# Where the split weights begin in their buffers, in the feed forwards of a two-layer decoder trunk

## The chip, the core and the metric

The kernel runs on one core of a Trainium2 chip. The metric is the device time of one execution in microseconds; the figure for the kernel before is the median of three runs. In the text TensorE (PE in the profile) multiplies matrices, and loading its weights is shown apart (PEld); VectorE is DVE, ScalarE is ACT, GpSimd is POOL, SyncE is SP.

## The reference

One sequence of 512 tokens, width 1024, goes through two layers. The first mixes with a gated DeltaNet, the second with sliding-window attention; both also attend to 256 memory tokens. After the mixing, each layer has a gated feed forward of width 2816. All in float32.

```python
def swiglu(h, w_gate_up, w_down):
    gu = h @ w_gate_up
    return (jax.nn.silu(gu[..., :D_FF]) * gu[..., D_FF:]) @ w_down

def reference(x, mem, ...):
    mem_n = rms_norm(mem, ln_mem)
    for layer in range(DEPTH):
        h = rms_norm(x, ln_mix[layer])
        mkv = mem_n @ w_mem_kv[layer]
        ...
        x = x + jnp.concatenate([mix_out.astype(x.dtype), mem_o.astype(x.dtype)], axis=-1) @ w_out[layer]
        x = x + swiglu(rms_norm(x, ln_ffn[layer]), w_gate_up[layer], w_down[layer])
        ...
    return rms_norm(x, ln_final)
```

## The kernel before, in words

**A product in three matmuls.** Every float32 operand of a large product is split into a high part and the rest (`split`, L168: ScalarE copies the high part into a float32r tile, L140, and VectorE subtracts it, L153). `mm3` (L198) then issues three matmuls for a tile of 128 by 128 weights: high weights by high inputs, high weights by the inputs' rest, the weights' rest by high inputs. In the profile they read `g<-h,whi`, `g<-l,whi`, `g<-h,wlo`: the moving operand first (the inputs, `h` and `l`, or `T`), then the weights. Each matmul loads its own weights (LDWEIGHTS in PEld).

**Where weights lie.** `weight` (L182) takes a block of weights that SP's queue has loaded into `wraw`, and splits it into a `whi` and a `wlo` tile of the pool `w`. `part` (L195) allots these with 1024 + 128 elements each, 128 more than a block fills. A block of eight tiles begins at the tile's first byte.

**The feed forward.** `ffn` (L1099) goes over the 22 pairs of gate and up columns in two halves of 11, and after each half multiplies the 11 results by the down weights. The first column of a half is done plainly with 512-wide matmuls (`projected`, `gate`). The others are done two at a time by `quarters` (L1275): one step of a fast method (Strassen-Winograd) over two blocks of columns, two halves of the input width and two halves of the tokens, seven products in place of eight. Each product is four tiles of weights times 256 tokens, so 4 × 3 = 12 matmuls that are 256 wide; their inputs are the normalised activations (`h`, `l`) or sums of them that were prepared at the start (`T`). VectorE forms the sums of weights and combines the results; GpSimd's queue adds weights to each other by accumulating DMAs. There are 19 calls of `quarters` in each feed forward, 1596 matmuls.

Their split weights come from `ring` (L1130): six places, each half of a `whi` and of a `wlo` tile, taken in turn. A place is 512 + 128 elements long, of which a product uses 512, beginning at element `shift[0]`. `begin` (L1139), which starts each call of `quarters`, sets `shift[0]` to `P - 8`, 120 elements or 480 bytes.

**The last rows.** In the second layer's last half the last two of eight blocks of rows are held back (`tail`), and done for 256 tokens at a time, so that normalising and storing the first half of the tokens runs beside the second half's products: 2 blocks × 2 halves × 11 tiles × 3 = 132 matmuls, 256 wide. Their weights are split to the beginning of `whi` and `wlo` tiles for the one block, of `T` tiles for the other.

**Positions.** In the built program each partition's `h`, `l` and `T` operands begin at 320 bytes beyond a multiple of 512, and so do `whi` and `wlo`; a further tile of weights is 512 bytes further on. The distance from the beginning of the weights to the beginning of the inputs, modulo 512, is therefore the same for all matmuls of a kind:

| matmuls | width | inputs beyond weights, bytes modulo 512 |
|---|---|---|
| quarter products, both feed forwards (3192) | 256 | 32 |
| last rows (132) | 256 | 0 |
| plain projections, all layers | 512 | 0 |
| memory keys, at the start (`mh`, `ml` as inputs, `whi` as weights) | 256 | 384 |
| memory values, at the start, with the roles exchanged (`whi` moving, `mh` as weights) | 256 | 128 or 416 |

The order of the work is that of the code; TensorE's instructions are issued in this order, and a place in the ring is written again when the matmuls that read it are done.

Of the kernel before, what the change touches and what calls it, by code (L numbers as in the profile page):

```python
# [18 lines left out]
P = 128  # L19
T = 512  # L20
D = 1024
KD = D // P
# [64 lines left out]
class Builder:  # L87
# [91 lines left out]
        self.loaded = self.nc.sync.dma_start(raw, src).ins  # L179
        return raw  # L180

    def weight(self, src, eng=None, raw=None, parts=1, pool=None, tags=("whi", "wlo"), bufs=3, after=None):  # L182

        raw = self.load(src) if raw is None else raw
        n = raw.shape[1]
        hi, lo = (self.part(tag, bufs, pool)[:, :n] for tag in tags)
        for i in range(parts):
            s = slice(i * n // parts, (i + 1) * n // parts)
            self.split(raw[:, s], hi[:, s], lo[:, s], eng or self.weng)
            if after is not None:  # L190
                for ins, other in zip((self.copied, self.low), after):
                    self.nosync(ins, other)
        return hi, lo
# [905 lines left out]
    def ffn(self, fp, xp, layer, h, apool, rope=False):  # L1099
# [4 lines left out]
        acts, sums, open_pairs, places, waiting, shift, sized = [], [], [], [], [], [0], []  # L1104
# [34 lines left out]
        def begin(f, up, by, tag, bufs, then):  # L1139

            o = [self.t(fp, [P, T], F32, tag, bufs) for _ in range(2)]
            steps = self.quarters(fp, [col(f + i, up) for i in range(2)], sums, by, o, ring)
            shift[0] = P - 8
            next(steps)
            while waiting:
                x = waiting.pop()
                self.nosync(self.fn(x, x, AF.Silu), self.held)
            end()
            next(steps)
            open_pairs.append((steps, then, o))  # L1150
            return o

        def end():
            if open_pairs:
                steps, then, o = open_pairs.pop()
                next(steps, None)
                for x in o:
                    then(x)

        def add(x, ps):  # L1160
            d = ps
            if not layer:
                d = self.t(fp, [P, T], F32, "fu", 3)
                self.tt(nc.vector, d, ps, self.rstd, ALU.mult)
            self.tt(nc.vector, x, d, x, ALU.add)

        for f0 in (0, half):
# [7 lines left out]
            for f in range(f0 + 1, f0 + half, 2):  # L1175
                if f == 1:
                    g = []
                    for i in range(2):
                        for _ in range(2 - i):
                            sums.append(self.token_sums(fp, layer, len(sums), h))  # L1180
                        g.append(gate(f + i))
                    sums.append(self.token_sums(fp, layer, len(sums), h))
                else:
                    g = begin(f, 0, (self.rstd, self.rstd), "fg", 4, lambda x: self.fn(x, x, AF.Silu))
                begin(f, 1, g, "fu", 3, put)
            end()
            self.acc = self.floor if layer else None
            tail = KD - 2 if f0 and layer else KD
            down = lambda m, j, n, **kw: self.weight(a["wdn"][layer, m][:, (f0 + j) * P:(f0 + j + n) * P], **kw)
            for m in range(tail):  # L1190
# [3 lines left out]
                for j, n in ((0, 6), (6, 5)):  # L1194
                    w = down(m, j, n)
# [7 lines left out]
        if tail < KD:  # L1203

            parts = (slice(0, T // 2), slice(T // 2, T))
            own = dict(pool=fp, tags=("T", "T"), bufs=8)
            w = {m: [down(m, j, n, **(own if m == KD - 1 else {})) for j, n in ((0, 6), (6, 5))] for m in range(tail, KD)}
            outs = [[self.t(fp, [P, D], F32, "T", 8) for _ in range(2)] for t in parts]
            for o, t in zip(outs, parts):
                for k in range(tail):  # L1210
                    self.put_row(o, k, self.x[k][:, t])
            ends = []
            for t in parts:
                acc = self.acc[:, t]
                for m in range(tail, KD):
                    ps, x = self.bank("pj")[:, :T // 2], self.x[m][:, t]
                    seeded = t.start > 0 and m == KD - 1
                    if seeded:
                        self.copy(ps, x)
                    for k in range(half):  # L1220
                        act = [part[:, t] for part in acts[k]]
                        self.mm3(ps, w[m][k // 6], k % 6, act, k == 0 and not seeded, k == half - 1, seeded)
                    if seeded:
                        x = ps
                    else:
                        add(x, ps)
                    if m < KD - 1:
                        sq = self.t(fp, [P, T], F32, "fg", 4)[:, t]
                        self.square(sq, x)
                        self.put_row(outs[len(ends)], m, x)  # L1230
                        nxt = self.t(xp, [P, T], F32, "sqa", 2)[:, t]
                        self.tt(nc.vector, nxt, acc, sq, ALU.add)
                        acc = nxt
                ends.append(self.final(fp, acc, x, outs[len(ends)], t, P if seeded else t.stop))
            for n, (end, o) in enumerate(zip(ends, outs)):
                self.store(*end, o, n)
# [381 lines left out]
```

## Time and profile before

| | |
|---|---|
| median of 3 runs | 1131.22 us (1130.96 to 1131.48) |
| the profiled execution | 1131.15 us, span 1129.4 us |
| TensorE, busy | 1119.9 us (99%) |
| weight loads, busy | 986.1 us (87%) |
| VectorE, busy | 827.6 us (73%) |
| ScalarE, busy | 634.4 us (56%) |
| granted TensorE clock | 0.998 |

The span runs from the first instruction to the last. A busy share is that of the whole span; matmuls are pipelined, so that one begins while the one before is still under way, and the length that a row gives for one matmul (some 280 ns for 256 columns) is longer than the distance from its beginning to the next one's beginning. What a matmul costs is this distance, called its spacing or step below; it is read from the length of a row in the chain of waits divided by its count, or from beginnings in the timeline.

### The profile page before, as it was taken

What the parts mean: (1) busy time and instruction counts of PE and PEld (TensorE: products, weight loads), DVE (VectorE), ACT (ScalarE), POOL (GpSimd) and SP (SyncE); (2) the same over time, 40 slices, a digit from 0 to 9 for tenths busy, and PEclk for the clock granted to TensorE, in tenths of its full rate; (3) what the DMA queues carried; (4) which work ended last, traced back from release to release, by engine and by line L of the source; (5) the groups of instructions that cost most, each with busy time, mean ns of one, the idle gap of its engine ahead of it and who ended that gap; (6) DMA issues with size and microseconds to landing.
All of it is one profiled execution on the core that took longest, in us unless ns stands there. A gap on an engine that the chain in (4) does not pass through costs nothing.

```text
span 1129.4 us, 19330 instructions
## 1 busy us (share of the span) xinstructions
PE 1119.9 (99%) x7339; PEld 986.1 (87%) x7339; DVE 827.6 (73%) x1553; ACT 634.4 (56%) x1285; POOL 73.2 (6%) x91
## 2 busy tenths in 40 slices
PE   9999999999999999999999999999999999999997
PEld 8888778887899988899988887788999988999986
DVE  7676976577888975588955877839999634889643
ACT  8588664456566632366643555856666422666434
POOL 0000000000021001011000000000111000111001
PEclk9999999999999999999999999999999999999999
DMA  8344252234567536377533321116687533776232
GB/s 314 109 153 149 95 131 86 85 113 145 174 167 195 143 111 169 102 191 195 134 89 102 132 75 38 53 43 180 158 201 185 144 103 105 173 190 156 77 103 87
DMA packets 72401, 151.15 MB, mean 134 GB/s; under 512 B 16956, under 2 KB 18516, under 8 KB 72308
## 3 DMA queue, kind: packets, MB, share of 16 engines
q1 hardware_dynamic: 60884, 129.21, 36.3%
q0 software_dynamic: 11136, 20.45, 11.2%
q8 instruction: 57, 0.93, 0.3%
q14 instruction: 36, 0.29, 0.1%
q10 hardware_dynamic: 288, 0.26, 0.1%
HBM read 142.94 MB, written 6.96 MB: 133 GB/s over the span
## 4 chain that ended last, share of the span: by engine, by line
PE 96%; DVE 2%; ACT 1%; DMA 0%; issue 0%; DVEq 0%; SPq 0%; ACTq 0%
PE pj L146 46%; PE g L146 38%; PE sc L146 6%; PE qk L146 3%; PE pt L146 2%; PE pt L150 1%; PE g L150 1%; DVE big L153 1%; DVE qv L156 0%; DVE btmp L153 0%; DMA early<-in_early 0%; DVE wlo L153 0%; ACT sm L134 0%; DVE T L153 0%; DVE gcr L153 0%
## 5 line engine op out<-in xcount | busy, mean ns | idle before, releaser
L140 ACT ACTIVATE whi<-wraw 128x512 fp32r<-128x512 f32 (+3 forms) x318 | 235.3, 748 | 240.6 <-PE pj L146 164.0
L153 DVE TENSOR_TENSOR wlo<-wraw,whi 128x512 fp32r<-128x512 f32 (+3 forms) x318 | 262.8, 837 | 92.7 <-ACT whi L140 85.2
L146 PE MATMUL pj<-h,whi 128*128 128x512 f32 (+1 forms) x652 | 256.4, 395 | 0.0
L146 PE MATMUL pj<-l,whi 128*128 128x512 f32 (+1 forms) x652 | 254.4, 390 | 0.0
L146 PE MATMUL pj<-h,wlo 128*128 128x512 f32 (+1 forms) x652 | 254.0, 390 | 0.0
L146 PE MATMUL g<-T,whi 128*128 128x256 f32 x1216 | 216.8, 279 | 0.0
L146 PEld LDWEIGHTS g<-T,whi 128*128 128x128 f32 x1216 | 185.1, 188 | 1.3 <-DVE fu L156 1.3
L146 PE MATMUL g<-T,wlo 128*128 128x256 f32 x608 | 169.7, 279 | 0.0
L146 PEld LDWEIGHTS pj<-h,whi 128*128 128x128 f32 x652 | 122.4, 188 | 28.0 <-issue 4.1
L146 PEld LDWEIGHTS pj<-h,wlo 128*128 128x128 f32 x652 | 122.5, 188 | 25.4 <-issue 0.9
L146 PE MATMUL g<-l,whi 128*128 128x256 f32 (+1 forms) x500 | 144.5, 289 | 0.0
L146 PE MATMUL g<-h,whi 128*128 128x256 f32 (+1 forms) x500 | 144.4, 289 | 0.0
L146 PE MATMUL g<-h,wlo 128*128 128x256 f32 (+1 forms) x500 | 144.4, 289 | 0.0
L146 PEld LDWEIGHTS pj<-l,whi 128*128 128x128 f32 x652 | 122.6, 188 | 23.6 <-DVE l L1468 0.3
L146 PEld LDWEIGHTS g<-T,wlo 128*128 128x128 f32 x608 | 114.3, 188 | 0.0
L146 PEld LDWEIGHTS g<-h,whi 128*128 128x128 f32 x500 | 94.0, 188 | 1.9
L146 PEld LDWEIGHTS g<-l,whi 128*128 128x128 f32 x500 | 93.9, 188 | 1.9
L146 PEld LDWEIGHTS g<-h,wlo 128*128 128x128 f32 x500 | 93.9, 188 | 1.8
L1286 POOL DMA_DIRECT2D ws<-in_wgu x38 | 33.5, 881 | 733.0 <-DMA ws<-in_wgu 399.1
L140 ACT ACTIVATE whi<-ws 128x512 fp32r<-128x512 f32 x76 | 48.0, 631 | 42.0 <-PE g L146 35.6
L153 DVE TENSOR_TENSOR wlo<-ws,whi 128x512 fp32r<-128x512 f32 x76 | 52.0, 684 | 5.9 <-ACT whi L140 5.9
L1287 POOL DMA_DIRECT2D ws<-in_wgu x38 | 34.2, 900 | 196.4 <-DVE wlo L153 71.4
(421 smaller groups left out, 1683.2 us busy)
## 6 DMA issues: line engine op xcount, KB each, us to landing
wraw<-in_wgu SPq DMA_DIRECT2D x50, 512.0 KB, 4.4
ws<-in_wgu SPq DMA_DIRECT2D x76, 256.0 KB, 3.4
ws<-in_wgu POOLq DMA_DIRECT2D x76, 256.0 KB, 4.5
wraw<-in_win SPq DMA_DIRECT2D x26, 512.0 KB, 3.6
wraw<-in_wdn SPq DMA_DIRECT2D x32, 384.0 KB, 3.1
wraw<-in_wdn SPq DMA_DIRECT2D x32, 320.0 KB, 2.9
wraw<-in_wgu SPq DMA_DIRECT2D x38, 256.0 KB, 4.0
wraw<-in_wout SPq DMA_DIRECT2D x16, 512.0 KB, 3.6
```

Source lines behind the costliest of these rows:

```text
L140: self.copied = self.nc.scalar.activation(out, in_, AF.Copy, **kw).ins
L146: return self.nc.tensor.matmul(out, lhsT, rhs, start=start, stop=stop, skip_group_check=more).ins
L150: return self.nc.tensor.transpose(out, in_, self.ident[:k, :k]).ins
L153: return eng.tensor_tensor(out=out, in0=a, in1=b, op=op).ins
L1286: nc.gpsimd.dma_start(s1, a22, accum_op=ALU.add)
L1287: nc.gpsimd.dma_start(s3, a21, accum_op=ALU.add)
```

## The change

The quarter products' weights begin elsewhere in their place of the ring: at element 80 (byte 320) in the first layer's feed forward and at element 16 (byte 64) in the second's, in both cases in place of element 120 (byte 480). `weight` gets an argument `at`, the element of the tile at which the split weights begin; the last rows' weights begin at element 80 in place of 0. So the inputs lie 192 bytes beyond the weights in the first feed forward (32 before), 448 in the second (32 before), and 192 in the last rows (0 before), modulo 512. The order of all engines' instructions and of the DMAs, their number and sizes, and the places of all other operands are the same as before.

```diff
-    def weight(self, src, eng=None, raw=None, parts=1, pool=None, tags=("whi", "wlo"), bufs=3, after=None):
+    def weight(self, src, eng=None, raw=None, parts=1, pool=None, tags=("whi", "wlo"), bufs=3, after=None, at=0):
 
         raw = self.load(src) if raw is None else raw
         n = raw.shape[1]
-        hi, lo = (self.part(tag, bufs, pool)[:, :n] for tag in tags)
+        hi, lo = (self.part(tag, bufs, pool)[:, at:at + n] for tag in tags)
...
             steps = self.quarters(fp, [col(f + i, up) for i in range(2)], sums, by, o, ring)
-            shift[0] = P - 8
+            shift[0] = 16 if layer else 80
             next(steps)
...
             own = dict(pool=fp, tags=("T", "T"), bufs=8)
-            w = {m: [down(m, j, n, **(own if m == KD - 1 else {})) for j, n in ((0, 6), (6, 5))] for m in range(tail, KD)}
+            w = {m: [down(m, j, n, at=80, **(own if m == KD - 1 else {})) for j, n in ((0, 6), (6, 5))] for m in range(tail, KD)}
```

## The prediction

> **What bounds the kernel.** I read the views in this order: cores, chain of waits, PE's timeline where two shapes can be compared, then the stage table of VectorE, which is next in line.
>
> The view of the cores and the page's first part:
>
> ```profile
> core 0: 1129.4 us, clock 0.998
> ...
> PE 1119.9 (99%) x7339; PEld 986.1 (87%) x7339; DVE 827.6 (73%) x1553; ACT 634.4 (56%) x1285; POOL 73.2 (6%) x91
> ```
>
> TensorE has something in flight for 1119.9 of 1129.4 us and its granted clock is 0.998, so it is TensorE's pace that sets the time, and what is left to win or lose is the spacing of its matmuls. The profiled execution took 1131.15 us (span 1129.4), 0.07 under the median of 1131.22, so a sum made against the span carries over to the median as it is.
>
> The chain of waits, in order of time (start, length, what, count), shows where that spacing can be read off:
>
> ```profile
> 17.29 3.60 PE sc L146 x30
> ...
> 26.65 5.81 PE pj L146 x48
> ...
> 318.53 86.80 PE g L146 x744
> 407.51 64.65 PE pj L146 x285
> 472.16 102.05 PE g L146 x852
> ...
> 801.60 86.80 PE g L146 x744
> 890.59 64.61 PE pj L146 x285
> 955.21 102.05 PE g L146 x852
> ...
> 1113.43 7.30 PE pj L146 x61
> ```
>
> The two x744 rows are quarter products alone: 86.80 / 744 = 116.7 ns from one 256-wide matmul to the next, without one gap. In the two x852 rows, 24 are 512-wide matmuls of one projection; at 64.65 / 285 = 226.8 ns they take 5.4 us, which leaves 96.6 us for 828, again 116.7 ns. So all quarter matmuls, 744 + 828 = 1572 of the 1596 of each feed forward, run at one pace (the remaining 24 stand in shorter pieces of the chain), and nothing but TensorE's own pace is on the path. In the last row, 256-wide matmuls of the last rows take 7.30 / 61 = 119.7 ns. That is 3 ns more for the same shape on the same engine. In the program they differ in the PSUM banks' tag and in the place of the operands: in the quarters the inputs lie 32 bytes beyond the weights (modulo 512), in the last rows 0. I call this distance the position.
>
> **The price of a position.** The change moves nothing else, so the whole forecast hangs on the spacing of 256-wide matmuls at 192 and at 448. No such position occurs in this trace. Others do. PE's timeline (start, modelled length, instruction) has, at position 0, the beginning of the last rows; at 384, the matmuls of the memory keys; at 128, those of the memory values, whose operands have their roles exchanged:
>
> ```profile
> 1103.66 0.28 PE L146 MATMUL pj<-h,whi 128*128 128x256 f32 x1
> ...
> 1104.38 0.28 PE L146 MATMUL pj<-h,whi 128*128 128x256 f32 x1
> ```
>
> ```profile
> 17.84 0.28 PE L146 MATMUL sc<-mh,whi 128*128 128x256 f32 x1
> ...
> 20.60 0.28 PE L146 MATMUL sc<-mh,wlo 128*128 128x256 f32 x1
> ```
>
> ```profile
> 21.70 0.28 PE L146 MATMUL sc<-ml,whi 128*128 128x256 f32 x1
> ...
> 23.48 0.28 PE L146 MATMUL sc<-ml,whi 128*128 128x256 f32 x1
> 23.61 0.28 PE L146 MATMUL sc<-mh,wlo 128*128 128x256 f32 x1
> ```
>
> ```profile
> 26.84 0.28 PE L146 MATMUL pj<-whi,mh 128*128 128x256 f32 x1
> ...
> 32.17 0.28 PE L146 MATMUL pj<-wlo,mh 128*128 128x256 f32 x1
> ```
>
> - Position 0: 6 steps from 1103.66 to 1104.38, 120.0 ns each (and 119.7 in the chain's x61).
> - Position 384: 23 steps from 17.84 to 20.60, 120.0 ns; in another stretch 16 steps from 21.70 to 23.61, 119.4 ns.
> - Position 128: 45 steps from 26.84 to 32.17, 118.4 ns.
> - Position 32: 116.7 ns, the lowest of all.
>
> Of the four positions with enough steps to be read, the three that are whole multiples of 64 bytes cost 118.4 to 120.0 ns, and the only one that is not, 32, is the only one below. 192 and 448 are both whole multiples of 64. They are read from their nearest neighbours: 192 lies nearest to 128 (118.4) and next to 384 (119.4 to 120.0), and I take 119.0 ns; 448 lies between 384 (119.7 as the mean of its two stretches) and 512, which is 0 again (120.0), and I take 119.9 ns. That four points make a rule, and that it is the 64 bytes and not the mere distance, is a guess; the neighbours give the same answer by either reading, which is why I choose it. The ends that I keep for one position are 118.4 and 120.3, the second a little above the worst row.
>
> In the Trainium skill, the page "SBUF — State Buffer", section "Who interferes with whom", gives TensorE two read ports that are independent, one for the moving operand and one for the weight load, and says that TensorE never waits on anyone. By that page a position is free, and the time would stay. The trace disagrees as far as it goes, 119.7 against 116.7 ns for the same shape; whether the reads of weights and inputs meet is not seen in any row.
>
> **The change part by part.**
>
> 1. First feed forward, quarter weights at byte 320 of their buffer in place of 480, so position 192 for 32. 1596 matmuls (19 pairs of columns, 7 products, 12 matmuls) by 119.0 − 116.7 = +2.3 ns: **+3.7 us**. All of it is on the path, since TensorE has no idle time there.
> 2. Second feed forward, byte 64, position 448. 1596 × (119.9 − 116.7) = 1596 × 3.2 ns: **+5.1 us**. Also on the path.
> 3. Last rows, byte 320 in place of 0, position 192 for 0. Two blocks of rows, two halves of tokens, 11 tiles, 3 matmuls: 132 × (119.0 − 120.0) = **−0.1 us**.
> 4. The splits write the same number of elements to another place in the same buffers. The rows by shape show whether the place costs anything on ScalarE or VectorE (the ones from ws go to byte 480, those of 768 and 640 elements nearly all to byte 0):
>
> ```profile
> L153 DVE TENSOR_TENSOR wlo<-ws,whi 128x512 fp32r<-128x512 f32 x76 | 52.0, 684 | 5.9 <-ACT whi L140 5.9
> L153 DVE TENSOR_TENSOR wlo<-wraw,whi 128x768 fp32r<-128x768 f32 x31 | 29.7, 957 | 7.8 <-ACT whi L140 7.6
> ...
> L153 DVE TENSOR_TENSOR wlo<-wraw,whi 128x640 fp32r<-128x640 f32 x31 | 25.5, 824 | 42.8 <-ACT whi L140 42.7
> ```
>
> From 768 to 640 elements the subtraction loses 133 ns; 128 fewer again would be 691, and 684 were measured at byte 480. The place costs these writers under 7 ns in an instruction of 684, and TensorE does not wait for them in the quarters. Cost: 0. The cover for it is VectorE's idle time there, in the table of stages below.
>
> Sum: 3.7 + 5.1 − 0.1 = +8.7 us. No wait, DMA, order or buffer changes, so no queue needs a term; a slower TensorE only loosens what VectorE, ScalarE and the DMAs must deliver.
>
> **How far the other way it could go.** If matmuls came closer together, VectorE would be next. Its busy time in two stretches that are quarters alone (the stretch, its length, busy time and count of instructions), and then PE's in the same two:
>
> ```profile
> 320.00:400.00 80.00, 72.86 (x132) 1.00 0.69 170
> ...
> 803.00:883.00 80.00, 75.47 (x139) 1.00 0.78 188
> ```
>
> ```profile
> 320.00:400.00 80.00, 80.00 (x688) 1.00 0.69 170
> ...
> 803.00:883.00 80.00, 80.00 (x689) 1.00 0.78 188
> ```
>
> VectorE works 72.86 / 688 = 105.9 ns for each matmul in the first feed forward and 75.47 / 689 = 109.5 in the second. Below that the gain of a better position would turn into waits for split weights. This bounds the gain at 1596 × (10.8 + 7.2) ns = 29 us and is no forecast. In the Trainium skill, the page "TensorE: Matmul & The Clock Gate", section "Back-to-back issue gap", gives N/2.4 + 2.5 ns, 109.2 for N = 256; if both positions reached that, an estimate by that page is 1106 us, and no row here is that fast.
>
> **The rivals.**
>
> - *Faster: 192 and 448 are better than 32.* Mechanism: two reads of one memory get out of each other's way as the distance grows, and 32 bytes is only the first step of that. For it: going from 0 to 32 gave 3.3 ns at once, and positions beyond 32 need not go back up before 128. Against it: 128 and 384 are worse than 32, and 448 lies between two rows of 119.4 to 120.0. It decides at a mean below 116.7 ns over both feed forwards. Price: one more such step, 113.3 ns, gives 3192 × −3.3 = −10.6 us, and 132 × −6.7 = −0.9 in the last rows: 1131.2 − 11.5 = 1119.7.
> - *No change.* The 3 ns have to do with the stage and not the place (other PSUM banks, a 512-wide neighbour), or one feed forward gains what the other loses. Then 1131.2, with at most 0.4 us from the last rows. Against it: positions 0, 128 and 384 in three stages all read above 116.7.
> - *Worse than any row.* At 192 both reads meet in mid matmul every time. The largest single step in the rows above is 0.13 us, rounded (23.48 to 23.61), so some 122 to 123 ns are seen singly; 122.5 ns as the mean of all would give 3192 × 5.8 = +18.6 us: 1149.8.
>
> **How the numbers follow.** Slower along the neighbours' rows 0.58, worse than any row 0.08, faster 0.26, no change 0.08. The likeliest gives 1131.2 + 8.7 = **1139.9**; by its own ends (118.4 and 120.3 for both) 3192 × 1.7 = +5.4 to 3192 × 3.6 = +11.5, so 1136.6 to 1142.7. The range for 8 in 10 takes in the faster rival at its one step and most of the worse one: 1120 to 1145, with about one in ten left out on either side. About 0.2%, 2.3 us, is what a measurement of this kernel can tell from no change. Faster by more than that 0.25; within it 0.08, into which a feed forward that gains against one that loses would also fall; slower by more 0.67.
>
> **What would show it.** In the profile after, the same chain has its rows x744: the first should last 744 × 119.0 = 88.5 us and the second 744 × 119.9 = 89.2, and the x852 rows 104.0 and 104.7, while the projection rows x285 stay at 64.6. The last rows' x61 should go from 7.30 to 7.26. If the first x744 row is under 86.8 and the second over, the two positions differ in sign and my neighbours' rule is wrong; if both are under, positions are not ruled by 64 bytes and the faster rival holds. If a quarter row shows idle time before TensorE, the forecast fails in another way: then writers, not reads, felt the place.

## The result and the profile after

The changed kernel takes 1134.42 us (median of 10 runs, 1131.59 to 1135.17) against 1131.22 for the kernel before (10 runs, 1130.90 to 1132.07): a ratio of 1.0025 with a 95% interval of 1.0016 to 1.0033. It is slower, by 3.2 us where 8.7 were forecast. Its runs spread over 3.6 us, three times as far as those of the kernel before. The profiled execution took 1133.86 us.

The view of the cores and the page's first part, after the change:

```profile
core 0: 1131.8 us, clock 0.998
...
PE 1122.4 (99%) x7339; PEld 990.1 (87%) x7339; DVE 829.2 (73%) x1553; ACT 634.8 (56%) x1285; POOL 73.1 (6%) x91
```

Clock and counts are as before; TensorE is busy 2.5 us longer. The chain of waits shows where (start, length, what, count):

```profile
318.06 87.63 PE g L146 x744
407.89 64.63 PE pj L146 x285
472.51 102.96 PE g L146 x852
...
802.72 87.63 PE g L146 x744
892.55 64.63 PE pj L146 x285
957.17 102.96 PE g L146 x852
...
1116.26 6.93 PE pj L146 x61
```

The x744 rows went from 86.80 to 87.63 us, the x852 rows from 102.05 to 102.96; the projections (x285) stayed. 87.63 / 744 is 117.8 ns a step, and (102.96 − 5.4) / 828 is 117.8 as well. Position 192 in the first feed forward and 448 in the second have the same step. The four stretches are 2 × 0.83 + 2 × 0.91 = 3.5 us longer. The span grew by 2.4 us only, mainly because the first x744 row began 0.47 us earlier than before and the last rows' x61 took 0.37 us less. That row fell from 7.30 to 6.93, to 113.6 ns a step, a pace below the 116.7 to 120.0 that the prediction had read in the kernel before. PE's timeline shows that the last rows' two halves of tokens, both at position 192, run at two paces:

```profile
1106.50 0.28 PE L146 MATMUL pj<-h,whi 128*128 128x256 f32 x1
...
1107.09 0.28 PE L146 MATMUL pj<-h,wlo 128*128 128x256 f32 x1
```

```profile
1116.57 0.28 PE L146 MATMUL pj<-h,whi 128*128 128x256 f32 x1
...
1117.14 0.28 PE L146 MATMUL pj<-h,wlo 128*128 128x256 f32 x1
```

Five steps in 0.59 us are 118.0 ns; ten microseconds later five steps in 0.57 us are 114.0, and they stay so to the end of the half (the times are rounded to 0.01 us; over 16 steps and more the two paces are 117.8 and 113.4). Same weights, same position, same shapes. This, and the neighbours' rule of the prediction, are what the experiments are about.

### The profile page after: what moved, and what is told of

The parts are those of the page before. It is cut to its first block, busy times and chain, and to the rows that moved or that the text cites. A ratio compares the mean times of both kernels' runs of the same rounds, so it can differ in the third digit from the quotient of the medians.

```text
span 1131.8 us, 19330 instructions
## 1 busy us (share of the span) xinstructions
PE 1122.4 (99%) x7339; PEld 990.1 (87%) x7339; DVE 829.2 (73%) x1553; ACT 634.8 (56%) x1285; POOL 73.1 (6%) x91
## 4 chain that ended last, share of the span: by engine, by line
PE 94%; DVE 3%; ACT 1%; DMA 1%; issue 0%; DVEq 0%; SPq 0%; ACTq 0%
PE pj L146 44%; PE g L146 39%; PE sc L146 6%; PE qk L146 3%; PE pt L146 2%; PE pt L150 1%; DVE big L153 1%; PE g L150 1%; DVE btmp L153 1%; DVE wlo L153 1%; ACT T L140 0%; DVE qv L156 0%; ACT sm L134 0%; DMA big<-basein 0%; DMA wraw<-in_wdn 0%
## 5 line engine op out<-in xcount | busy, mean ns | idle before, releaser
L146 PEld LDWEIGHTS g<-T,whi 128*128 128x128 f32 x1216 | 187.7, 190 | 1.2 <-DVE fu L156 1.2
```

What stands on the lines that cost most here:

```text
L146: return self.nc.tensor.matmul(out, lhsT, rhs, start=start, stop=stop, skip_group_check=more).ins
```

## The experiments

Three theories stood against each other. **A**: the rule of 64 bytes, as the prediction has it. **B**: each position has its own step, by the distance of the two operands. **C**: one position allows several steady paces, and how a stretch begins chooses among them.

### Every position on a grid of 32 bytes

```diff
-            shift[0] = P - 8
+            shift[0] = 8 * ((7 * calls[0] + 3 if layer else calls[0]) % 16)
+            calls[0] += 1
```

> The kernel before, with a new position for each of the 19 calls of quarters in a feed forward: the weights begin at 0, 8, 16, ... 120 elements in turn in the first feed forward, in another order (steps of 7) in the second. So each of the 16 positions that are multiples of 32 bytes is held twice for about 84 matmuls. Theory A (the rule of 64 bytes, as the prediction put it): odd multiples of 32 give 116.7 ns a step, multiples of 64 give 117.8 to 120. Theory B (distance): the step is a smooth curve over 512 bytes, alike for neighbours, with 32 near its low end and 192 and 448 at 117.8. Theory C (several steady paces at one position, and the start of a stretch chooses): the same position has different steps in the two feed forwards, 113.3 among them, as in the second half of the last rows after the change.

It took 1139.22 us in one run. The steps below are worked out from PE's timeline: the beginnings of the first and the last matmul at a position, divided by the steps between (71 or 83). Stretches with a wait in them are left out. Positions p and p + 256 are put together: where a position had one step, the two agreed to 0.2 ns. At 32, 160 and 192, which had several, p and p + 256 have one step in common (117.8, 118.8 and 117.8); the others were read on one side alone, 113.4 and 113.5 at 192 and not at 448, for instance (the grid of 4 bytes below has 113.5 at 448).

```
position modulo 256   steps in ns, in order of time
  0                   119.9 119.9 119.9 120.0
 32                   117.8 117.8 117.8 116.7
 64                   117.8 117.8 117.8 117.8
 96                   119.9 119.9 120.0 120.0
128                   118.6 118.6 118.7 118.7
160                   117.4 120.0 117.3 118.8 118.8
192                   117.8 113.4 117.8 117.8 117.8 113.5
224                   118.3 118.3 118.3 118.4 118.4
```

Rows of PE's timeline for three stretches at 192, the first and last matmul of each:

```profile
487.11 0.28 PE L146 MATMUL g<-h,whi 128*128 128x256 f32 x1
...
496.52 0.28 PE L146 MATMUL g<-T,wlo 128*128 128x256 f32 x1
```

```profile
812.19 0.28 PE L146 MATMUL g<-h,whi 128*128 128x256 f32 x1
...
821.97 0.28 PE L146 MATMUL g<-T,wlo 128*128 128x256 f32 x1
```

```profile
1044.89 0.28 PE L146 MATMUL g<-h,whi 128*128 128x256 f32 x1
...
1054.31 0.28 PE L146 MATMUL g<-T,wlo 128*128 128x256 f32 x1
```

83 steps take 9.41, 9.78 and 9.42 us. Theory A falls: 64 and 192 are about as good as 32, while 96 is an odd multiple of 32 and as bad as 0. Theory B holds within this scan for five of the eight positions, with a period of 256 bytes on this grid, though not as a smooth curve; 32, 160 and 192 had more than one step each, as theory C has it. Position 32, at which the kernel before ran all its long stretches at 116.7 ns, ran at 117.8 in three stretches of four here.

### A grid of 4 bytes

```diff
-            shift[0] = P - 8
+            shift[0] = 19 * layer + calls[0]
+            calls[0] += 1
```

> As the scan by 32 bytes, in steps of one element: the weights begin at element 0, 1, 2, ... 18 in the first feed forward's 19 calls, at 19 to 37 in the second's. Theory A: the step repeats every 64 bytes (16 calls), with its best at 32 modulo 64. Theory B: no repetition within 152 bytes, neighbours differ by under 0.3 ns. Theory C: jumps between the same few paces (113.3, 116.7, 117.8, 118.6, 120.0) in no order of the position.

It took 1135.01 us in one run, with 38 positions from 512 down to 364, read by the same working. All but four lie between 115.7 (504) and 122.2 (404), and neighbours 4 bytes apart differ by up to 6.5 ns (428: 120.0, 424: 113.5). Four ran at 113.5 to 113.7: 460, 448, 436 and 424. They lie 12 bytes apart, but the next at that distance on either side, 472 and 412, ran at 119.2 and 119.8. No repetition by 64 bytes, and no smooth curve: theory A falls again, and B in its smooth form.

### The 512-wide matmuls

```diff
-                    w = down(m, j, n)
+                    w = down(m, j, n, at=8 * ((m + 8 * (f0 > 0) + 5 * layer) % 16))
```

> The kernel before, with the down weights' blocks (512-wide matmuls) beginning at a multiple of 8 elements that changes with the block of rows, so that the positions 0, 32, ... 480 all occur; quarters stay at 32. Before, at position 0, the step is 226.7 ns. Theory A: odd multiples of 32 bytes come under 226.7 (by some 3 ns, 223.4, as in the quarters), multiples of 64 stay. Theory B: a curve over 512 bytes. Theory C, or weight loads being what the position acts through: a 512-wide matmul leaves a load twice the time, so the step stays at 226.7 everywhere.

It took 1135.89 us in one run. The chain's row of the first down products:

```profile
407.25 66.02 PE pj L146 x285
```

It was 64.65 us with all weights at position 0. By the timeline, the mean step of a row of blocks (33 matmuls, rows with a wait left out) was 226.7 ns at 0 and 256, 228.8 to 229.2 at 64 and 320, and 232.2 to 234.0 at all others. So the position acts on a matmul whose step is twice as long, too, and there 0 and 256 are the best of this grid. The bet in the third theory that it would stay at 226.7 is refuted.

### The changed kernel once more

> The changed kernel once more, for the steps in another execution of it. Theories A and B: both feed forwards at 117.8 ns again, the last rows as in the first profile, 117.8 and then 113.3. Theory C: some stretch is at another pace than in the first profile, 113.3 or 116.7 in place of 117.8 or the reverse, and the time differs by the matmuls in it (828 at 4.4 ns is 3.7 us).

Its chain has the quarters as before to the hundredth (87.63 twice, 102.96 twice), while the last rows are back at the slower pace, 7.18 / 61 = 117.7 ns:

```profile
1116.53 7.18 PE pj L146 x61
```

It took 1134.38 us. The same program is not at the same pace everywhere in two executions; here it was only the last rows, worth 0.25 us in that row.

### Another way into position 448

Two kernels that differ in the position of the first call of `quarters` in each half alone; all other calls are at 448. The last of a call's seven products is split after the next call has begun and takes that call's position, so 72 of the first call's 84 matmuls have the other position.

```diff
-            shift[0] = P - 8
+            shift[0] = 16 if calls[0] else 8
+            calls[0] += 1
...
             places.clear()
+            calls[0] = 0
```

> The kernel before with the first call of quarters in each half of a feed forward at position 480 and all others at 448 (480 and 448 are the same as 224 and 192 modulo 256 in the scan). In the scan a stretch at 192 that came from 480 or 224 ran at 113.4 ns and one that came from 416 at 117.8. Theory C: the 2856 matmuls at 448 run at 113.3 to the end of each half, the 336 at 480 at 118.4: 2856 x -3.33 + 336 x +1.7 = -8.9 us, 1122.3. Theories A and B: 448 has one step, 117.8, as in the changed kernel: 1131.2 + 3.6 = 1134.8.

The second has 24 in place of 8.

> The same with the first call of each half at position 416 in place of 480. Theory C: the other way in, so the matmuls at 448 run at 117.8 again, about 1134.5. If the step at 448 is 113.3 here too, it is any change of position, and not the one it comes from, that chooses the pace: 1122.

The first took 1125.26 us (5 runs, 1123.71 to 1126.51), a ratio of 0.9950 (0.9936 to 0.9963); the second 1133.67 us in one run. Chain of waits of the first:

```profile
317.80 84.68 PE g L146 x744
...
796.49 87.24 PE g L146 x744
...
950.55 94.22 PE g L146 x804
```

and of the second:

```profile
317.77 87.60 PE g L146 x744
...
802.40 87.60 PE g L146 x744
...
956.79 102.93 PE g L146 x852
```

At one and the same position, 672 matmuls of the first half run at 113.3 ns when the call before them was at 480, and at 117.8 when it was at 416. (84.68 us = 72 × 118.3 + 672 × 113.3 ns; the first 72 are at 480.) In each profile all four halves agree: every one began at 113.3 behind 480, and at 117.8 behind 416. That is theory C, and B alone cannot give it. What chooses is not the position before by itself, as my expectation had it: the scan by 32 bytes went from 480 to 448 twice and ran at 117.8 both times, and its stretch at 1044.89 us came from 416 and ran at 113.5. Some finer state of the stream at the change must decide, which these runs don't show.

The row of 87.24 us is a half in which the fast pace was lost on the way. PE's timeline of the first kernel there:

```profile
804.84 0.28 PE L146 MATMUL g<-h,whi 128*128 128x256 f32 x1
...
817.08 0.45 PE L146 MATMUL g<-T,whi 128*128 128x256 f32 x2
817.37 0.28 PE L146 MATMUL g<-T,wlo 128*128 128x256 f32 x1
...
883.45 0.28 PE L146 MATMUL g<-T,wlo 128*128 128x256 f32 x1
```

108 steps from 804.84 to 817.08 are 113.3 ns each. Then two steps take 0.29 us, some 0.06 too long, and the 561 steps from 817.37 to 883.45 are 117.8 ns each. A stall of 60 ns thus went with 561 × 4.4 ns = 2.5 us. That accounts for most of the 3.0 us between the expected 1122.3 and the measured 1125.26. No row of this trace says what the stall waited for. VectorE had just read the bank of results (PSUM) that the late matmul writes:

```profile
816.49 0.43 DVE L156 SCALAR_TENSOR_TENSOR fg<-g,fs 128x256 f32<-128x256 f32 x1
```

It ended at 816.92, 0.16 us before the matmul at 817.08. At the same place in the code the profiles of the next kernel and of the one with position 436 throughout name this operation as what TensorE waited for; here that is likely and not shown.

### Two fine positions over whole feed forwards

```diff
-            shift[0] = P - 8
+            shift[0] = 22 if layer else 19
```

> The kernel before with the quarters at position 436 in the first feed forward and 424 in the second, both no multiples of 32; in the scan by 4 bytes each ran at 113.4 ns, once. Theory B (a position has its step): 3192 x -3.3 = -10.5 us, 1120.7. Theory C: entered from a 512-wide stretch and not from a neighbouring position, they may take another pace, 116.7 to 120.0; then 1131 to 1142.

1124.04 us (4 runs, 1122.52 to 1125.19), a ratio of 0.9939 (0.9925 to 0.9953). Chain of waits:

```profile
317.79 84.34 PE g L146 x744
...
816.30 66.04 PE g L146 x564
```

Position 436 gives 84.34 / 744 = 113.4 ns in the first feed forward, entered straight from 512-wide matmuls. In the second, position 424 began at 113.3, met a stall of 0.31 us that ends at 816.30 (the chain has VectorE's `fg` of L156 just before it), and ran on at 66.04 / 564 = 117.1 (by single steps 116.7 after a short transition). The second half was at the fast pace again. So both positions allow the fast pace, and 424 allows a slower one too. The result lies between theory B's 1120.7 and theory C's 1131: three halves of four kept the fast pace, and the slower steps of the fourth, 564 × 3.4 ns, are 1.9 us of the difference.

### Distance or place

```diff
         s = self.t(cp, [P, 24], F32, "small")
+        self.t(cp, [P, 8], F32, "pad")
```

> The kernel before with 32 bytes of padding ahead of the weights, so that the weights, x, h and l lie 32 bytes further on, and T and what lies behind it stay. Quarter matmuls with h or l keep position 32, those with T get position 0; projections of h keep position 0, those of ac8 to ac10 get 480. If the distance decides: h projections stay at 226.7 ns, the products with h at about 116.7 and those with T at 120.0, mean 118.6, and matmuls of ac8 to ac10 go to 233. If the place itself modulo 64 decides: h projections leave 226.7.

1140.43 us in one run. PE's timeline, a projection of `h`, and quarter products with `T`; below them the chain's first x744:

```profile
598.72 0.39 PE L146 MATMUL pj<-h,wlo 128*128 128x512 f32 x1
...
600.08 0.39 PE L146 MATMUL pj<-h,wlo 128*128 128x512 f32 x1
```

```profile
329.07 0.28 PE L146 MATMUL g<-T,whi 128*128 128x256 f32 x1
...
329.91 0.28 PE L146 MATMUL g<-T,wlo 128*128 128x256 f32 x1
```

```profile
318.43 88.55 PE g L146 x744
```

The projections, moved together with their weights, keep 1.36 / 6 = 226.7 ns. The matmuls with `ac8` to `ac10` in the same rows of blocks, whose weights moved alone, went from 226.7 to 233.6, about the 233 that was expected. The products with `T`, whose weights moved and whose inputs did not, have 0.84 / 7 = 120.0, the step of position 0. The mean of the quarters is 88.55 / 744 = 119.0. So for the 512-wide matmuls it is the distance that decides, and not where in memory the two lie, and the `T` products agree. The products with `h` do not show it as cleanly: at an unchanged distance they had 116.8 to 118.3, 118.0 on the mean, and not the 116.7 of before. They follow `T` products every few matmuls and may have taken another pace of position 32 (117.8 in the scan); that is not shown.

### Position 436 throughout

```diff
-            shift[0] = P - 8
+            shift[0] = 19
...
-            w = {m: [down(m, j, n, **(own if m == KD - 1 else {})) for j, n in ((0, 6), (6, 5))] for m in range(tail, KD)}
+            w = {m: [down(m, j, n, at=19, **(own if m == KD - 1 else {})) for j, n in ((0, 6), (6, 5))] for m in range(tail, KD)}
```

> Position 436 for the quarters of both feed forwards and for the last rows. Theory C with 436 as a position at which 113.3 ns holds best: 3192 x -3.33 = -10.6 and 132 x -6.7 = -0.9 us, less what VectorE's lateness costs in the second feed forward's first half, where one short wait ended the pace at 448 and at 424: 1119.5 to 1123, steps of 113.3 outside that half. If a short wait knocks 436 out of its pace too, that half (744 matmuls) shows 113.3 at first and 116.7 to 120 after the wait.

1120.90 us (4 runs, 1120.69 to 1121.30) beside 1131.34 for the kernel before, measured together with it: a ratio of 0.9909 (0.9892 to 0.9926). It beats both kernels. Chain of waits:

```profile
318.07 84.33 PE g L146 x744
...
816.65 64.17 PE g L146 x564
...
947.65 93.87 PE g L146 x804
...
1103.36 6.92 PE pj L146 x61
```

113.3 to 113.8 ns in every row (in the row x804, 24 are 512-wide and take 5.4 us). The stall near 816 us is there too, and at 0.37 us longer than in the other kernels. The 564 matmuls behind it have 64.17 / 564 = 113.8 on the mean, and by single steps they are back at 113.3 within three steps. The rows by shape name what TensorE waited for, in the last column; the kernel before, then this one:

```profile
L146 PE MATMUL g<-T,whi 128*128 128x256 f32 x1216 | 216.8, 279 | 0.0
```

```profile
L146 PE MATMUL g<-T,whi 128*128 128x256 f32 x1216 | 211.4, 277 | 0.5 <-DVE fg L156 0.2
```

So the stall is a wait for VectorE, a wait that the kernel before does not have: TensorE reaches the bank sooner at the faster pace. Its four runs lie within 0.6 us, where those at 448 and at 436 with 424 spread over 2.7 to 2.8.

### A grid of 8 bytes for the 512-wide matmuls

```diff
-                    w = down(m, j, n)
+                    w = down(m, j, n, at=2 * (m + 8 * (f0 > 0) + 16 * layer))
```

> The kernel before with the down weights (512-wide matmuls) beginning at element 0, 2, 4, ... 58, one row of blocks each, so the position falls from 512 by 8 bytes a row. The scan by 32 bytes had 226.7 at 0 as the lowest, 229.0 at 64 and 231.7 to 234 at the others. If 512-wide matmuls have positions off the 32-byte grid that are better, as 436 is for 256-wide ones, some row is under 226.7; if a weight load is what such a position helps, none is, since a 512-wide matmul leaves a load time enough.

It took 1136.40 us in one run. No row of blocks was clearly under 226.7 ns. 0 and 392 were at 226.6 to 226.8, 320 at 228.5 over its last matmuls; all others, from 504 to 280, had means between 230.1 and 234.3. There is nothing to win for the 512-wide matmuls on this grid; positions off it were not tried.

## Why the prediction was off

**What bounds the kernel** held: TensorE's spacing sets the time, and a change of 1.1 ns in one step came out as 3.5 us in the chain. So did the part on the writers: ScalarE and VectorE did not feel the place (DVE 827.6 to 829.2 us busy), and no new wait arose in the quarters. VectorE came next, as the prediction said, but sooner than its mean of 109.5 ns a matmul suggests: at 113.3 TensorE already waited for it at one place, and there for its reading of a bank, not for split weights.

**The price of a position** is the step that failed. The prediction read 192 and 448 from their nearest neighbours, 128, 384 and 0, took 119.0 and 119.9 ns, and got +3.7 and +5.1 us. Measured: 117.8 ns at both, +1.1 ns × 3192 = +3.5 us. The sign was right and the term mis-sized, by more than a factor of two. The reason is not a small error of reading. Neighbours were no guide: even those on the finer grid of 32 bytes differ (192, with 113.4 to 117.8, lies between 160 with 117.3 to 120.0 and 224 with 118.3), and the rule of 64 bytes, called a guess there, is refuted by 64 and by 96. So the sign was luck: it came from the paces that the two kernels happened to hold, 116.7 at position 32, which the scan has at 117.8 as well, and 117.8 at 192 and 448, which have 113.3 as well. My ends for one position, 118.4 and 120.3, left out the measured value altogether.

**The mechanism behind it** was thought of as a step that belongs to a position. The trace of before had a hint that I passed over: position 384 read 120.0 in one stretch and 119.4 in another, and I took the mean of the two. (The second, 16 steps from rounded times, is good to some 0.6 ns; unrounded it is 118.9. The scan has 118.6 to 118.7 at 384.) The reading of 128 was loose as well: the table of positions gives 128 or 416 for that stretch. The runs show that one position can have several steady paces, 113.3 and 117.8 at 192 and 448 among them.

**The last rows** were forecast at −0.1 us for 120.0 to 119.0. In the row x61 the change brought −0.37 us in the one profile and −0.12 in the other, by which pace they took.

**The rivals.** The faster one, a further step to 113.3 ns, named a pace that exists at this very position; the last rows ran at it, and the kernel with another first call ran most of its quarters at it. It did not come about because the changed kernel's quarters entered the slower pace in all eight long stretches of its two profiles. No change is refuted: only the place of the weights changed, and the step ranged from 113.3 to 122.2 ns. In the Trainium skill, "SBUF — State Buffer" ("Who interferes with whom") says that TensorE never waits on anyone; the prediction's reading of it, that a position is free, does not hold here, while what inside TensorE takes the time is in no row. The 109.2 ns that "TensorE: Matmul & The Clock Gate" ("Back-to-back issue gap") in the Trainium skill gives for an isolated matmul were reached by no stretch here; 113.3 was the fastest.

**What stays open.** Why the steps repeat every 256 bytes, and what picks the pace when a stretch begins, was not settled. That the stall made the pace change at 448 and at 424 rests on the order in time, once each. The ten runs of the changed kernel go down to 1131.59 us; one stretch of 744 matmuls at 113.3 instead of 117.8 would be 3.3 us less and could explain it, but that execution was not profiled.

## What to carry to other kernels

Where TensorE is the bound, its steps depend on the distance between the beginnings of moving operand and weights, here by up to 9 ns in 117, and a scan that changes the distance call by call inside one kernel reads dozens of distances from one profile. Don't infer one distance from another, and don't take a distance by its best stretch: look for one that has the good pace in every stretch, and that comes back to it after a stall. A faster step also brings waits for the next engine before that engine's mean is reached. A kernel whose runs spread wider than those of its relative may be falling between two paces.

## What the runs showed of the hardware that was not expected

- A pace lasts: 744 matmuls in a row at 113.4 (position 436), 116.7 (32) or 117.8 ns (192 and 448), and two executions of the changed kernel have 87.63 us in all four rows of 744.
- Behind a stall of 60 ns one pace gave way to another for 561 matmuls (113.3 to 117.8 at position 448); at 436, behind a stall of 0.37 us, 113.3 came back.
- On the grid of 32 bytes the effect repeats with 256 bytes, and it is there for 512-wide matmuls as well (226.7 to 234.3 ns), with other positions as the best ones: 0 is among the worst for 256 columns on that grid (119.9 to 120.0) and the best for 512 (226.7).
